# A residual gate's matrix-vector product moved from TensorE to VectorE, and a branch projection split in two, in a hybrid block on one core

## The chip, the cores and the metric

One core of one Trainium2 chip runs the whole block in one launch. The metric is device microseconds of one execution: the median of the kernel before is 1565.91 us (three runs, 1564.96 to 1569.58).

## The reference

One layer (DEPTH is 1) over 256 context and 256 latent tokens with D_MODEL 2048. Only the latent stream is returned, so the context is used as keys, values and seed states alone. Cut to what matters here:

```
shift, scale, gate = split(silu(c) @ w_mod + b_mod, 3)          # c is one vector of 2048
h      = rms_norm(x) * (1 + scale) + shift                      # 512 tokens, context first
parts  = split(h @ w_in)                                        # 3 mixers' inputs, 3 x 2048 merge logits
y_na   = neighbourhood attention, 16 heads of 64                # latent queries, latent and context keys
y_pool = multiscale pooling, 4 channel groups of 256
y_rw   = RWKV-7 scans in both directions, 16 heads of 64, latent seeded by context
b_i    = y_i * silu(gate_i)                                     # 256 x 1024 each, i = 0, 1, 2
merged = sum over i of sigmoid(logits_i) * (b_i @ w_branch[i])  # 1024 -> 2048
out    = rms_norm(x + gate * (merged @ w_out)) * final_g
```

All is fp32. The residual gate is a product of one vector of 2048 with a 2048 x 2048 part of w_mod (16.8 MB), plus a bias.

## The kernel before

There are three stages. The first (up to about 150 us of the profiled execution) computes shift and scale, turns x, builds h in 16 K tiles (`hh`, `hl`) and already multiplies seven column tiles. The second ("mixers", to about 1470 us) does all else up to `merged`. The third multiplies by w_out and writes the result.

Matrix products of fp32 numbers are made of three products each: a number is split into a rounded high part (cast on ScalarE, L576) and a remainder (subtraction on VectorE, L577), and high x high, low x high, high x low are accumulated (`mm3`, L580 to L584, and L856).

In the mixers weights are read in units of 512 KB (`load_unit`, three `raw` buffers); a unit is split in two halves (`split_half`, five buffers for each part), and every half gives some matmuls. There are four kinds of work for these units. `column_tile` (L835) multiplies h with 128 columns of w_in: queries, keys, values and gates of a pair of attention heads, inputs and gates of the pooling and of a pair of RWKV heads. `merge_group` (L955), twelve of them, multiplies the latent part of h with 512 columns of the merge logits over 16 K tiles (96 matmuls of 512 columns), takes a tanh (half of the sigmoid) and stores it in DRAM (`md_`). `branch_group` (L959), three branches by four column groups, multiplies a branch's output, 8 K tiles (48 matmuls), with w_branch, and multiplies in the merge gate, which it reads back from `md_` (`gates_in`, with the third of its four units). The branch outputs go to DRAM (`bs`, by `keep`, L882) and come back as K tiles in the places of hh and hl when h isn't needed any more (`branch_load`, L618). The fourth kind are the gate units.

`gate_units` (L1105) computes the residual gate: 32 units of eight matmul instructions. Each multiplies a [128, 32] tile of `cs` (the two conditioning vectors and zeros) with 256 columns of the gate's weights (`wg`, loads of 256 KB) for four K tiles, each in a column group of its own of the array. A matmul with the matrix `selg` (L1100) then sums the four groups over partitions and spreads the row over 128 partitions, the bias is added, and the result goes to DRAM (`gd`) until the last stage.

`Order` (L447) writes out TensorE's order by hand, as a plan of the program in which every piece of work has a cost in us and streams have due times: the attention and pooling of the pairs one after the other (`side`, first priority), the last sums' transposes (`turn`), and the RWKV pairs (`rwkv`), in which features, a triangular inverse (VectorE), an 8-step chain and a readout follow each other, and the next pair's start overlaps. After at most 2.2 us of streams comes at least 0.6 us of units. Units are prepared three halves ahead. `todo` (L1137) lists the tiles in their order, each with the event it waits for; the first that is free is taken, and a merge group always is (the last one is held back until nothing else is left). The tiles of attention pair p wait for `side{p-1}`. When `todo` is empty come the branch groups, in order; those of the third branch wait for `rw7`, the output of the last RWKV pair. Gate units are added to two of three halves once `side7` is there. The framework that lowers the program orders the other engines' instructions and the loads (nearly all DMAs are issued from SP) and puts in the waits.

Of the kernel before, what the change touches and what calls it, by code (L numbers as in the profile page):

```python
# [446 lines left out]
class Order:  # L447
# [48 lines left out]
    def run(s, units, most, least):  # L496

        while True:
            s.bursts(most)
            n = 0.0  # L500
            while n < least:
# [5 lines left out]
                if u is None:  # L507
                    nxt = [x[1] for x in s.streams if x[2] is None] + [s.ev[x[2]] for x in s.streams if x[2] in s.ev]
# [7 lines left out]
D = 2048  # L516
# [13 lines left out]
def hybrid_block(ctx, tc, x, cx, w_ms, w_st, w_in, w_mg, w_br, w_out, pool_w, icnt, wa, bias, rows, params, out, dbg=None):  # L530
# [81 lines left out]
    def branch_st(br):  # L612
        def st(k):
            c = slice(256 * (k % 2), 256 * (k % 2) + 256)
            return hh[4 * br + k // 2][:, c], hl[4 * br + k // 2][:, c]
        return st

    def branch_load(i):  # L618

        br, k = i // 4, 2 * (i % 4)  # L620
        for e, y in enumerate((hh, hl)):
            x = y[i] = hp.tile([P, 512], F32R, tag=f"h{'hl'[e]}{i}", name=f"b{'hl'[e]}{i}")
            nc.sync.dma_start(x.bitcast(F32).rearrange("p (k t) -> p k t", k=2), bs[br, e, k:k + 2].rearrange("k p t -> p k t"))

    def branch_src(br, c):
        return lambda u: w_br[br, 4 * c:4 * c + 4, :, 256 * u:256 * u + 256].rearrange("n p c -> p n c")
# [6 lines left out]
    sums = {}  # L633
# [17 lines left out]
    with ExitStack() as sx:  # L651
# [11 lines left out]
        selg = cp.tile([P, P], F32, name="selg")  # L663
        nc.gpsimd.memset(selg, 0.0)
        for g in range(4):
            r = slice(32 * g, 32 * g + 32)
            nc.gpsimd.affine_select(out=selg[r], in_=selg[r], pattern=[[0, P]], compare_op=ALU.not_equal, fill=1.0,
                                    base=-1, channel_multiplier=1)
# [197 lines left out]
    with ExitStack() as mx:  # L866
# [7 lines left out]
        T = {}  # L874
# [7 lines left out]
        def keep(br, p, b):  # L882
# [4 lines left out]
            nc.sync.dma_start(bs[br, 0, p], h.bitcast(F32))  # L887
            nc.sync.dma_start(bs[br, 1, p], l.bitcast(F32))
# [61 lines left out]
        def merge_out(i, t, d):  # L950
            th = wp.tile([P, 512], F32, tag="mt", bufs=2, name=f"mth{i}_{t}")
            nc.scalar.activation(th, d, AF.Tanh, scale=0.5)  # L952
            nc.sync.dma_start(md_[i, t], th)
# [5 lines left out]
        def branch_group(br, c):  # L959
            th = {}  # L960

            def gates_in(u):
                for t in range(2):
                    th[t] = wp.tile([P, 512], F32, tag="mt", bufs=2, name=f"bth{br}_{c}_{t}")
                    nc.sync.dma_start(th[t], md_[4 * br + c, t])
                return u()

            def done(t, a):
                o = merged(t, c) if br == 0 else th[t]
                nc.vector.scalar_tensor_tensor(o, th[t], 1.0, a, ALU.add, ALU.mult)  # L970
                if br:
                    nc.vector.tensor_tensor(merged(t, c), merged(t, c), o, ALU.add)
# [4 lines left out]
            return us  # L977

        def turn(c):
            yield 0.0, 2.0  # L980
# [5 lines left out]
        def rwkv(p):  # L986
# [33 lines left out]
            keep(2, p, g)  # L1020
            O.mark(f"rw{p}")
# [74 lines left out]
        def gate_out(cc, gs, gb):  # L1096
            yield 0.0, 1.2
            c = slice(512 * cc, 512 * cc + 512)
# [6 lines left out]
        def gate_units():  # L1105

            held = []

            def load(cc, h, k):
                wg = np_.tile([P, 2, 256], F32, tag=("kt", "sl")[k // 2 % 2], bufs=2 + k // 2 % 2, name=f"wg{cc}_{h}_{k}")  # L1110
                nc.sync.dma_start(wg, w_mg[cc, k, :, :, 256 * h:256 * h + 256])
                held.append(wg)
                if k % 2 == 0:
                    return []

                def mult():
                    if h == 0 and k == 1:
                        T["mg"] = psn.tile([P, 512], F32, tag="s", name=f"mg{cc}")
# [221 lines left out]
```

## Time and profile before

| | |
|---|---|
| median of 3 runs | 1565.91 us |
| profiled execution | 1570.13 us, span 1568.4 us |
| TensorE matmul busy | 1509.2 us (96%), 12248 instructions |
| VectorE busy | 1129.1 us (72%), 2588 instructions |
| ScalarE busy | 798.9 us (51%), 1597 instructions |
| GpSimd busy | 243.5 us (16%), 436 instructions |
| DMA | 289.26 MB, mean 184 GB/s |
| chain that ended last | PE 81%, DVE 7%, DMA 5%, ACT 4%, issue 3% |

PE is TensorE, DVE VectorE, ACT ScalarE, POOL GpSimd, SP the engine that issues most DMAs. Busy times of an engine are shares of the span from its first to its last instruction; matmuls are pipelined, so that their durations overlap. The chain follows the last instruction back, at each step to what released it.

### The profile page before, as it was taken

What the parts mean: (1) busy time and instruction counts of PE and PEld (TensorE: products, weight loads), DVE (VectorE), ACT (ScalarE), POOL (GpSimd) and SP (SyncE); (2) the same over time, 40 slices, a digit from 0 to 9 for tenths busy, and PEclk for the clock granted to TensorE, in tenths of its full rate; (3) what the DMA queues carried; (4) which work ended last, traced back from release to release, by engine and by line L of the source; (5) the groups of instructions that cost most, each with busy time, mean ns of one, the idle gap of its engine ahead of it and who ended that gap; (6) DMA issues with size and microseconds to landing.
All of it is one profiled execution on the core that took longest, in us unless ns stands there. A gap on an engine that the chain in (4) does not pass through costs nothing.

```text
span 1568.4 us, 32279 instructions
## 1 busy us (share of the span) xinstructions
PE 1509.2 (96%) x12248; PEld 1197.0 (76%) x12248; DVE 1129.1 (72%) x2588; ACT 798.9 (51%) x1597; POOL 243.5 (16%) x436
## 2 busy tenths in 40 slices
PE   6999999999999999999999999999999997999998
PEld 4667778788877897788789877877896664666787
DVE  4334688788788777886887778768877775666674
ACT  5224563566365546544664556446646642334553
POOL 2222010040023023201230130023023200210000
PEclk9999999999999999999999999999999999999999
DMA  9996445555543464344355524623566698877863
GB/s 391 348 330 219 143 135 169 146 160 182 159 144 98 132 177 148 100 132 121 99 165 164 166 90 123 189 103 112 172 193 217 193 309 260 273 253 250 285 220 106
DMA packets 218380, 289.26 MB, mean 184 GB/s; under 512 B 62576, under 2 KB 176368, under 8 KB 213616
## 3 DMA queue, kind: packets, MB, share of 16 engines
q1 hardware_dynamic: 218224, 287.20, 57.1%
q8 instruction: 96, 1.57, 0.4%
q14 instruction: 60, 0.49, 0.1%
HBM read 265.38 MB, written 21.50 MB: 183 GB/s over the span
## 4 chain that ended last, share of the span: by engine, by line
PE 81%; DVE 7%; DMA 5%; ACT 4%; issue 3%; SPq 0%; ACTq 0%; POOL 0%; DVEq 0%; POOLq 0%
PE d L856 32%; PE dg L582 8%; PE dg L583 7%; PE dg L584 7%; PE acc L780 2%; PE o L584 2%; PE o L582 2%; PE o L583 2%; DVE wlo L577 2%; PE px L374 1%; PE pu L388 1%; PE acc L786 1%; PE acc L783 1%; PE pS L398 1%; DMA raw<-in_w_br 1%
## 5 line engine op out<-in xcount | busy, mean ns | idle before, releaser
L576 ACT CAST whi<-raw 128x512 fp32r<-128x512 f32 x584 | 355.1, 619 | 395.0 <-PE d L856 163.5
L577 DVE TENSOR_TENSOR wlo<-raw,whi 128x512 fp32r<-128x512 f32 x584 | 401.1, 698 | 142.2 <-ACT whi L576 113.7
L856 PE MATMUL d<-hh,whi 128*128 128x256 f32 (+1 forms) x1184 | 366.5, 329 | 0.9 <-ACT mth L952 0.9
L856 PE MATMUL d<-hl,whi 128*128 128x256 f32 (+1 forms) x1184 | 358.1, 322 | 0.0
L856 PEld LDWEIGHTS d<-hh,whi 128*128 128x128 f32 x1184 | 224.8, 190 | 24.1 <-issue 2.9
L856 PE MATMUL d<-hh,wlo 128*128 128x256 f32 (+1 forms) x1184 | 241.4, 323 | 0.0
L856 PEld LDWEIGHTS d<-hl,whi 128*128 128x128 f32 x1184 | 225.2, 190 | 16.2 <-issue 0.2
L856 PEld LDWEIGHTS d<-hh,wlo 128*128 128x128 f32 x1184 | 182.7, 190 | 17.0 <-issue 0.7
L582 PE MATMUL dg<-whi,hh 128*128 128x512 f32 x384 | 164.2, 428 | 5.4 <-DVE gnag L896 3.6
L370 POOL TENSOR_SCALAR sg<-SV,G 64x64 f32<-64x64 f32 x192 | 109.1, 574 | 362.1 <-DVE SV L407 201.0
L584 PE MATMUL dg<-wlo,hh 128*128 128x512 f32 x384 | 151.0, 393 | 0.3 <-DVE wlo L577 0.3
L583 PE MATMUL dg<-whi,hl 128*128 128x512 f32 x384 | 151.2, 394 | 0.0
L582 PE MATMUL dg<-whi,bh 128*128 128x512 f32 x192 | 83.9, 437 | 11.9 <-ACT whi L576 8.5
L582 PEld LDWEIGHTS dg<-whi,hh 128*128 128x128 f32 x384 | 72.1, 188 | 28.8 <-issue 5.3
L584 PEld LDWEIGHTS dg<-wlo,hh 128*128 128x128 f32 x384 | 72.4, 189 | 17.2 <-DVE wlo L577 0.7
L583 PEld LDWEIGHTS dg<-whi,hl 128*128 128x128 f32 x384 | 72.6, 189 | 9.8
L584 PE MATMUL dg<-wlo,bh 128*128 128x512 f32 x192 | 77.2, 402 | 1.4 <-DVE wlo L577 1.4
L583 PE MATMUL dg<-whi,bl 128*128 128x512 f32 x192 | 77.0, 401 | 0.8 <-DMA bl<-bs 0.8
L309 DVE TENSOR_TENSOR iM<-iA,iT 128x126 f32<-128x126 f32 (+22 forms) x248 | 63.3, 255 | 12.9 <-DMA iA<-dA 6.5
L311 DVE TENSOR_TENSOR iT<-iT,iM 128x126 f32<-128x126 f32 (+22 forms) x248 | 63.2, 255 | 6.7
L793 ACT ACTIVATE hh<-xT,md 128x256 fp32r<-128x256 f32 x32 | 17.5, 593 | 88.1 <-DVE md L708 88.1
L582 PEld LDWEIGHTS dg<-whi,bh 128*128 128x128 f32 x192 | 37.0, 192 | 30.6 <-ACT whi L576 12.0
(323 smaller groups left out, 2480.0 us busy)
## 6 DMA issues: line engine op xcount, KB each, us to landing
raw<-in_w_in SPq DMA_DIRECT2D x244, 512.0 KB, 3.7
wm<-in_w_ms SPq DMA_DIRECT2D x32, 1024.0 KB, 5.9
raw<-in_w_br SPq DMA_DIRECT2D x48, 512.0 KB, 5.2
wg<-in_w_mg SPq DMA_DIRECT2D x64, 256.0 KB, 4.4
raw<-in_w_out SPq DMA_DIRECT2D x32, 512.0 KB, 4.3
wst<-in_w_st SPq DMA_DIRECT2D x16, 448.0 KB, 7.1
md__79<-mth SPq DMA_DIRECT2D x24, 256.0 KB, 3.0
bth<-md__79 SPq DMA_DIRECT2D x24, 256.0 KB, 3.7
```

The costliest lines, as they stand in the source:

```text
L309: nc.vector.tensor_tensor(m, A[:, st:st + 1, st + 1:32].to_broadcast([128, ni, nt]), T[:, 0:ni, st:st + 1].to_broadcast([128, ni, nt]), AL ...
L311: nc.vector.tensor_tensor(T[:, 0:ni, st + 1:32], T[:, 0:ni, st + 1:32], m, ALU.add)
L370: nc.gpsimd.tensor_scalar(sg[hv[par], d], SV[hv[par], par, w, d], G[hv[par], gs[d][0], d:d + 1], None, ALU.mult)
L374: nc.tensor.matmul(px[hv[par], d], EO[:, par, d, cs[d], :], SV[:, par, w, d], start=True, stop=True, tile_position=(0, 64 * par))
L576: nc.scalar.copy(hi, src)
L577: nc.vector.tensor_tensor(lo, src, hi.bitcast(F32), ALU.subtract)
L582: nc.tensor.matmul(acc, a[0], b[0], start=start, stop=False)
L583: nc.tensor.matmul(acc, a[1], b[0], start=False, stop=False)
L584: nc.tensor.matmul(acc, a[0], b[1], start=False, stop=stop)
L780: mm = nc.tensor.matmul(acc[i], shi[:, c], hh[j], start=(j == 0), stop=False)
L793: nc.scalar.activation(hh[j][:, c], xT[:, j, c], AF.Identity, bias=mds[j][:, 0, e:e + 1], scale=mds[j][:, 1, e:e + 1])
L856: nc.tensor.matmul(box[0], w[m >= 8][:, 128 * i:128 * i + 128], x, start=(v == 0 and m == 0), stop=(v == 3 and m == 11))
```

## The change

The gate's products leave TensorE. `gate_piece` multiplies one K tile of 512 columns of the gate's weights by the conditioning value of each partition and adds it to a running [128, 512] sum: one operation on VectorE per K tile, 16 for a block of 512 columns, 64 in all, each with a load of 256 KB into one of two buffers (tag `kt`). A block is begun when the attention and pooling of pairs 1, 3, 5 and 7 are done (`side1`, ...), with one piece for every half unit. A matmul with a matrix of ones then sums over partitions and spreads. The attention tiles of pairs 2, 4 and 6 now wait for the block before them (`gate0` to `gate2`).

The third branch is projected in two parts of four K tiles: the first parts of all four column groups wait for `rw5`, the second ones for `rw7`. Each part is multiplied by the merge gate by itself and added; the additions of the second parts are on POOL but for the last group. The gate tiles for the second parts are fetched earlier into buffers that are free by then (`ahead`). `gates_in` comes with the last unit of a group instead of the third.

The last RWKV pair's output is split and stays in SBUF (`T["last"]`); K tile 7 of branch 3 is read from there. Operands of the third branch are loaded from `rw6` on, with every second unit. `gd`, `md_` and `bs` become separate DRAM tiles, and the stores of `md_` and of the high parts of `bs` are issued from ScalarE's queue.

```diff
-    gd = drp.tile([P, D], F32, name="gd")
-    md_ = drp.tile([12, 2, P, 512], F32, name="md_")
-    bs = drp.tile([3, 2, 8, P, NT], F32, name="bs")
+    gd = [drp.tile([P, 512], F32, name=f"gd{i}") for i in range(4)]
+    md_ = [drp.tile([2, P, 512], F32, name=f"md{i}_") for i in range(12)]
+    bs = [[drp.tile([2, P, NT], F32, name=f"bs{b}_{e}_{k}") for k in range(4)] for b in range(3) for e in range(2)]
...
-    def branch_st(br):
+    def branch_st(br, k0=0):
         def st(k):
+            k += k0
+            if br == 2 and k == 7:
+                return T["last"]
...
-            nc.sync.dma_start(bs[br, 0, p], h.bitcast(F32))
-            nc.sync.dma_start(bs[br, 1, p], l.bitcast(F32))
+            nc.scalar.dma_start(bs[2 * br][p // 2][p % 2], h.bitcast(F32))
+            nc.sync.dma_start(bs[2 * br + 1][p // 2][p % 2], l.bitcast(F32))
...
+            def ahead(u):
+                for t in range(2):
+                    tag, n = (("kt", 2), ("sl", 3), (("sl", 3), ("vT", 1))[t], ("mt", 2))[c]
+                    pool = wp if tag == "mt" else np_
+                    x = gates2[c, t] = pool.tile([P, 512], F32, tag=tag, bufs=n, name=f"cth{c}_{t}")
+                    nc.sync.dma_start(x, md_[8 + c][t])
+                return u()
...
+                    (nc.gpsimd if part == 2 and c < 3 else nc.vector).tensor_tensor(merged(t, c), merged(t, c), o, ALU.add)
-                if br == 2 and t and c < 3:
+                if part == 2 and t and c < 3:
                     O.add(turn(c), 1)
-            us = group(8, branch_src(br, c), branch_st(br), done)
-            us[2] = lambda u=us[2]: gates_in(u)
+            if part == 2:
+                us = group(4, branch_src(br, c, 2), branch_st(br, 4), done)
+                if c == 3:
+                    us[0] = lambda u=us[0]: ahead(u)
+                return us
+            us = group(4 if part else 8, branch_src(br, c), branch_st(br), done)
+            us[-1] = lambda u=us[-1]: gates_in(u)
+            if part and c < 3:
+                us[1] = lambda u=us[1]: ahead(u)
             return us
...
+            if p < 7:
+                keep(2, p, g)
+            else:
+                h = wp.tile([P, NT], F32R, tag="th", bufs=1, name="lasth")
+                l = np_.tile([P, NT], F32R, tag="ql", name="lastl")
+                nc.scalar.copy(h, g)
+                nc.vector.tensor_tensor(l, g, h.bitcast(F32), ALU.subtract)
+                T["last"] = h, l
+            O.mark(f"rw{p}", 1.5 * (p == 7))
...
+        def gate_out(cc, gs):
+            gb = np_.tile([P, 512], F32, tag="vT", name=f"gb{cc}")
+            nc.sync.dma_start(gb, rows[0:1, 512 * cc:512 * cc + 512].to_broadcast([P, 512]))
+            yield 0.0, 2.0
             pg = psn.tile([P, 512], F32, tag="o", name=f"pg{cc}")
-            nc.tensor.matmul(pg, selg, gs, start=True, stop=True)
+            nc.tensor.matmul(pg, ones, gs, start=True, stop=True)
             nc.vector.tensor_tensor(gb, pg, gb, ALU.add)
-            nc.sync.dma_start(gd[:, c], gb)
+            nc.sync.dma_start(gd[cc], gb)
             yield 1.1, 0.0
+            O.mark(f"gate{cc}")
+        def gate_piece(cc, kt):
+            wg = np_.tile([P, 512], F32, tag="kt", bufs=2, name=f"wg{cc}_{kt}")
+            nc.sync.dma_start(wg, w_mg[cc, kt // 2, :, kt % 2])
+            if kt == 0:
+                gs[cc] = np_.tile([P, 512], F32, tag="sl", bufs=3, name=f"gs{cc}")
+                nc.vector.tensor_scalar(gs[cc], wg, cs[:, kt, 1:2], None, ALU.mult)
+            else:
+                nc.vector.scalar_tensor_tensor(gs[cc], wg, cs[:, kt, 1:2], gs[cc], ALU.mult, ALU.add)
+            if kt == 15:
+                O.add(gate_out(cc, gs[cc]), 1)
...
-            na = f"side{p - 1}" if p else None
+            na = (f"gate{p // 2 - 1}" if p % 2 == 0 else f"side{p - 1}") if p else None
...
-        late = [(br, c) for br in range(3) for c in range(4)]
+        late = [(br, c) for br in range(2) for c in range(4)] + [(2, c, part) for part in (1, 2) for c in range(4)]
...
-                            elif not todo and late and (late[0][0] < 2 or O.has("rw7")):
+                            elif not todo and late and (len(late[0]) < 3 or O.has(("rw5", "rw7")[late[0][2] - 1])):
...
-                            if last >= 18 and loads and O.has("rw7"):
+                            if last >= 18 and last % 2 == 0 and loads and O.has("rw6"):
                                 branch_load(loads.pop(0))
...
-                    if n % 3 and O.has("side7") and gates and not 4 <= (last or 0) < 9:
-                        ready[-1] = ready[-1] + gates.pop(0)()
+                    if gates and O.has(f"side{2 * gates[0][0] + 1}"):
+                        gate_piece(*gates.pop(0))
```

## Rows read from the trace of the kernel before

**Rows 1.** Windows by stage: us, busy (instructions) of PE, PEld, DVE, ACT, POOL; clock, DMA share, GB/s.

```profile
160.00:1160.00 1000.00, 981.81 (x8553) 813.60 (x8552) 795.01 (x1868) 558.02 (x1149) 163.63 (x323) 1.00 0.46 141
...
1260.00:1340.00 80.00, 69.17 (x470) 47.85 (x468) 50.58 (x122) 25.09 (x44) 0.00 (x0) 0.96 0.92 279
...
1420.00:1480.00 60.00, 56.19 (x248) 45.06 (x248) 41.06 (x72) 28.11 (x53) 0.00 (x0) 0.97 0.89 293
```

**Rows 2.** Instructions grouped by line, PE: busy us, mean ns; idle before.

```profile
L1123 PE MATMUL mg<-wg,cs 128*32 128x256 f32 x256 | 20.4, 391 | 0.0
```

**Rows 3.** Timeline of PE around one gate unit: start us, us, instruction.

```profile
1401.58 0.40 PE L584 MATMUL dg<-wlo,bh 128*128 128x512 f32 x1
1401.91 0.64 PE L1123 MATMUL mg<-wg,cs 128*32 128x256 f32 x8
1402.48 0.50 PE L582 MATMUL dg<-whi,bh 128*128 128x512 f32 x1
1402.82 0.40 PE L583 MATMUL dg<-whi,bl 128*128 128x512 f32 x1
1403.06 0.40 PE L584 MATMUL dg<-wlo,bh 128*128 128x512 f32 x1
1403.29 0.40 PE L582 MATMUL dg<-whi,bh 128*128 128x512 f32 x1
```

**Rows 4.** Timeline of PE, the longest wait: idle before and its releaser in brackets.

```profile
1321.85 0.80 PE L582 MATMUL dg<-whi,bh 128*128 128x512 f32 x1 [4.37 <-ACT whi L576]
```

**Rows 5.** Windows inside the late stretch.

```profile
1286.00:1300.00 14.00, 11.83 (x57) 7.66 (x58) 12.71 (x37) 4.57 (x8) 0.00 (x0) 1.00 1.02 333
...
1324.00:1332.00 8.00, 8.00 (x91) 5.72 (x91) 4.35 (x7) 2.89 (x6) 0.00 (x0) 0.77 0.86 261
```

**Rows 6.** Timeline of DVE and PE where the last RWKV pair ends.

```profile
1419.11 0.42 DVE L1019 SCALAR_TENSOR_TENSOR grwg<-y,grwg 128x256 f32<-128x256 f32 x1
...
1427.61 0.47 PE L582 MATMUL dg<-whi,bh 128*128 128x512 f32 x1 [1.28 <-ACT whi L576]
1428.90 0.50 PE L583 MATMUL dg<-whi,bl 128*128 128x512 f32 x1 [0.82 <-DMA bl<-bs]
```

**Rows 7.** Timeline of PE, SP and ACT at a border of two branch groups.

```profile
1445.86 0.47 PE L582 MATMUL dg<-whi,bh 128*128 128x512 f32 x1 [0.76 <-DVE bth L970]
...
1448.69 1.49 SPq L564 DMA_DIRECT2D raw<-in_w_br  x2
...
1453.87 1.16 ACT L576 CAST whi<-raw 128x512 fp32r<-128x512 f32 x2 [1.56 <-DMA raw<-in_w_br]
```

**Rows 8.** Timeline of DVE: three remainders in a row.

```profile
370.22 1.88 DVE L577 TENSOR_TENSOR wlo<-raw,whi 128x512 fp32r<-128x512 f32 x3
```

**Rows 9.** Windows of 35 to 44 us after each second attention pair's pooling.

```profile
357.00:392.00 35.00, 35.00 (x288) 28.66 (x287) 29.71 (x60) 21.94 (x44) 0.61 (x1) 1.00 0.61 185
593.00:634.00 41.00, 40.77 (x397) 32.05 (x397) 32.84 (x76) 26.46 (x56) 13.80 (x27) 1.00 0.47 147
866.00:910.00 44.00, 44.00 (x397) 34.65 (x396) 32.77 (x67) 24.89 (x50) 9.14 (x18) 1.00 0.52 170
1173.00:1215.00 42.00, 42.00 (x431) 29.10 (x433) 30.05 (x67) 25.96 (x53) 12.49 (x21) 1.00 0.70 224
```

**Rows 10.** Line L1111, the 64 loads of the gate's weights: time to landing.

```profile
DMA to landing us min/median/max: 3.0/4.4/7.9
```

**Rows 11.** Timeline of ACT: the last pooling tile's tanh, the next merge group's.

```profile
354.31 0.39 ACT L894 ACTIVATE thplg<-d 128x256 f32<-128x256 f32 x1
...
384.56 0.60 ACT L952 ACTIVATE mth<-dg 128x512 f32<-128x512 f32 x1 [0.63 <-PE dg L584]
```

**Rows 12.** Timeline of ACT: tanh of the ninth and tenth merge groups.

```profile
1100.95 1.09 ACT L952 ACTIVATE mth<-dg 128x512 f32<-128x512 f32 x2
...
1203.70 0.60 ACT L952 ACTIVATE mth<-dg 128x512 f32<-128x512 f32 x1 [0.47 <-PE dg L584]
```

**Rows 13.** Waits of SP: line, for whom, us in total, times, longest.

```profile
SPq L887 <- ACT kh L884: 48.7, 21, 6.0
```

More of the change, by code (lines that the diff above doesn't have):

```diff
@@ L507, in run @@
                 if u is None:
-                    nxt = [x[1] for x in s.streams if x[2] is None] + [s.ev[x[2]] for x in s.streams if x[2] in s.ev]
+                    nxt = [x[1] for x in s.streams if x[2] is None] + [s.ev[x[2]] for x in s.streams if x[2] in s.ev] \
+                        + [v for v in s.ev.values() if v > s.t] * (not s.streams)
                     assert nxt, [x[2] for x in s.streams]
@@ L632, in merged @@
         return sums[t, c]
-    sums = {}
+    sums, T = {}, {}
     mhl = {}
@@ L662, in hybrid_block @@
         nc.vector.tensor_tensor(cs[:, :, 1], csil[:, 16:32], pp[:, PC_C + 16:PC_C + 32], ALU.mult)
[L663 to L668, printed above, removed]
+        ones = cp.tile([P, P], F32, name="ones")
+        nc.gpsimd.memset(ones, 1.0)
         xT = xp.tile([P, 16, 512], F32, name="xT")
@@ L873, in hybrid_block @@
         O = Order(tc)
-        T = {}
         def ztile(tag, nm, n):
@@ L952, in merge_out @@
             nc.scalar.activation(th, d, AF.Tanh, scale=0.5)
-            nc.sync.dma_start(md_[i, t], th)
+            nc.scalar.dma_start(md_[i][t], th)
         def merge_group(i):
@@ L957, in merge_group, with branch_group @@
             return group(16, src, lambda k: (hh[k][:, 256:512], hl[k][:, 256:512]), lambda t, d: merge_out(i, t, d))
-        def branch_group(br, c):
+        def branch_group(br, c, part=0):
             th = {}
@@ L1101, in gate_out @@
             nc.vector.tensor_tensor(gb, pg, gb, ALU.add)
-            nc.sync.dma_start(gd[:, c], gb)
+            nc.sync.dma_start(gd[cc], gb)
             yield 1.1, 0.0
[L1105 to L1118, printed above, removed]
-                    a = T["mg"][:, 256 * h:256 * h + 256]
-                    for i in range(4):
-                        kt = 2 * k - 2 + i
-                        g = kt % 4
-                        nc.tensor.matmul(a[32 * g:32 * g + 32], cs[:, kt], held[i // 2][:, i % 2], start=(kt < 4), stop=(kt >= 12),
-                                         tile_position=(0, 32 * g), skip_group_check=True)
-                    del held[0:2]
-                    if h == 1 and k == 7:
-                        gs = np_.tile([P, 512], F32, tag="sl", bufs=3, name=f"gs{cc}")
-                        gb = np_.tile([P, 512], F32, tag="sl", bufs=3, name=f"gb{cc}")
-                        nc.scalar.copy(gs, T["mg"])
-                        nc.sync.dma_start(gb, rows[0:1, 512 * cc:512 * cc + 512].to_broadcast([P, 512]))
-                        O.add(gate_out(cc, gs, gb), 1)
-                    return 0.75
-                return [mult]
-            return [lambda cc=cc, h=h, k=k: load(cc, h, k) for cc in range(4) for h in range(2) for k in range(8)]
@@ new lines, in gate_out @@
+            O.mark(f"gate{cc}")
+        gs = {}
+        def gate_piece(cc, kt):
[8 more added lines that the diff above has]
+                O.add(gate_out(cc, gs[cc]), 1)
@@ L1162, in hybrid_block @@
             todo.append((None, lambda i=i: merge_group(i)))
-        late = [(br, c) for br in range(3) for c in range(4)]
+        late = [(br, c) for br in range(2) for c in range(4)] + [(2, c, part) for part in (1, 2) for c in range(4)]
         def units():
-            ready, halves, cur, gates = [], [], [], gate_units()
+            ready, halves, cur = [], [], []
+            gates = [(cc, kt) for cc in range(4) for kt in range(16)]
             n = 0
@@ L1252, in hybrid_block @@
         cs_ = slice(512 * cc, 512 * cc + 512)
-        late = ((gate[:, cs_], gd[:, cs_]), (xr[0][:, cs_], x[0:128, cs_]), (xr[1][:, cs_], x[128:256, cs_]),
+        late = ((gate[:, cs_], gd[cc]), (xr[0][:, cs_], x[0:128, cs_]), (xr[1][:, cs_], x[128:256, cs_]),
                 (fg[:, cs_], rows[1:2, cs_].to_broadcast([P, 512])))
```

25 lines of the change are left out of this document (12 added, 13 removed).

## The prediction

> **What bounds the kernel now.** I read the busy time by stage first. TensorE is busy for 981.8 of the 1000 us of the mixers, but for 69.2 of the 80 us from 1260 to 1340, and 56.2 of the 60 from 1420 to 1480 [rows 1]. The order of its instructions is fixed when the kernel is built, and it works through them in that order. So the time is its work plus its idle time, and a change earns what it takes from either. The idle time that lies late is the first thing to see: 10.8 us between 1260 and 1340, in the stretch in which the gate's weights (64 loads), the branch weights and the branch operands are all being fetched. There the DMA share is 0.92, and VectorE isn't full.
>
> **What the gate's products cost TensorE.** Of the group, the reader is to see 256 instructions, 391 ns each, and only 20.4 us busy [rows 2]: four column groups run at once, and each unit is eight instructions. The timeline gives the price of one unit. Between two products of a branch group lie 0.23 us from start to start (1403.06 to 1403.29); across a unit they lie 0.90 us apart (1401.58 to 1402.48), and the next one comes 0.34 instead of 0.23 us later [rows 3]. That is 0.67 + 0.11 = 0.78 us a unit, and 32 units make 25.0 us. The bounds are 20.4 (busy alone) and 25.0; I take 25.0, since starts hold the gaps too. The Trainium skill (Perfetto Trace Analysis, Identifying the Most-Contended Engine) warns that busy time of matmuls is a poor measure because they are pipelined. The trace agrees: the 256 durations add up to 100 us, the busy time is 20.4 and the starts say 25.0; by the busy time the sum below would gain 4.6 us less.
>
> The four sums over partitions stay (a matrix of ones instead of the selecting one, same shape): no change.
>
> **What the late stretch gives back.** The longest single wait of TensorE, 4.37 us ahead of 1321.9, is for the high part of a branch weight [rows 4], and the DMA share was 1.02, at 333 GB/s, from 1286 to 1300 [rows 5]. Three quarters of the gate's 16.8 MB leave this part of the kernel. Idle: 10.8 us. The clock was granted at 0.77 from 1324 to 1332, right after that idle time [rows 5]; 8 us x 0.23 = 1.8 us of work. Together 12.6 us go, if what replaces the gate loads doesn't saturate the queues again (below).
>
> **What the last pair's wait gives back.** TensorE waits 1.28 and 0.82 us at 1427 to 1429, the second for the operand read back from DRAM [rows 6]. With that operand in SBUF, and three of its four neighbours loaded from rw6 on, 2.1 us go. The split of the third branch adds no product: 4 groups of 8 K tiles become 8 of 4. It moves 4 x 24 products x 0.23 = 22 us ahead of the last pair. Without it, taking out 25 us of gate units would leave TensorE short of filler: the last chain's final product on VectorE starts at 1419.1 [rows 6], the second branch's fillers last to about 1427, so 8 us are left over; 8 + 22 - 25 = 5 us still are. Next late is then the chain of the last pair itself. Four more group borders, each with a wait like the 0.76 us at 1445.9 [rows 7], at most 3 us, at least 0; I take 1, as most borders show none.
>
> **What the pieces on VectorE cost.** 64 operations of 128x512, fp32; the nearest rows are the low parts of weights, three in 1.88 us, 0.63 each [rows 8]. 40 us of VectorE in four blocks of 16, 10.1 us a block. In the stretches where the blocks will fall (after the pooling of each second head pair) VectorE is busy 29.7 of 35, 32.8 of 41, 32.8 of 44 and 30.1 of 42 us [rows 9]. With 10.1 more the first is over by 4.8, the second by 1.9; the others fit. TensorE, which has no idle time there to give (35.0 of 35, 40.8 of 41), stalls for what is over, 6.7 us, and for chain steps that stand behind a piece on VectorE. The bounds are 0 (weights are split three halves ahead) and 39: a piece's load waits for the piece two before it, since two buffers hold them; a load lands in 4.4 us [rows 10], so two pieces take 4.4 + 0.63 = 5.0 us, 2.5 a half unit, and a merge group of 16 half units takes 30.2 us (354.3 to 384.6), 1.89 each [rows 11]; 64 x 0.61 = 39. I take 10, nearer to the full-engine count, because the late loads' 4.4 was measured where the queues are full. Behind a waiting load stand the weight loads on SP; behind a waiting piece, every chain step on VectorE.
>
> Moved by this: the tiles of head pairs 2, 4 and 6 wait for a block. A block is 16 half units, as long as a merge group, so each pair can come up to 30 us later, and merge groups fill in. Nine of the twelve are done at 1102, the tenth at about 1205 [rows 12], so there are just enough; cost 0, at worst one group short, 22 us (96 products x 0.23).
>
> **What the new order of loads costs.** In the first parts of branch 3 the gate tiles are fetched with the second of two units, behind the read of the group before. The rows of a group of today: first product at 1445.86, the weights' load behind the gate tiles' at 1448.69, their cast at 1453.87 [rows 7], so the unit behind the gates is ready 8.6 us after the border (0.6 for the cast). Today two units (5.5 us) and the turned sums cover that; then one unit does, 4 x 3 x 0.23 = 2.8 us. Bounds per group: 0 (the weights may be issued ahead, chain steps fill in) to 5.8; four groups, 0 to 23 us. I take 7, a third, since chain steps lie between there and the load will be faster with the gate's loads gone. In the eight groups of branches 1 and 2 the gates move to the last of four units, which is included in the 12.6.
>
> Branch operands (0.5 MB for every second unit), weights (0.5 MB a unit of 2.76 us) and gate tiles (0.5 MB a group of 11 us) still ask for about 95 + 190 + 47 = 332 GB/s, as much as the best stretch moved [rows 5]. Bounds 0 to 10.8; I take 4, for two groups instead of six.
>
> At nothing: stores issued on ACT (ACT is off the path; SP spent 48.7 us waiting ahead of the kept operands' stores alone [rows 13], hidden by three weight buffers; -3 to 3, the latter if the casts of weights come late behind them), six additions on POOL (hidden by the next group's products; the transposes behind them would wait some tenths more without these), DRAM tiles apart (0 to -2).
>
> **Sum.** Gone 25.0 + 12.6 + 2.1 = 39.7. Added 10 + 7 + 4 + 1 = 22. Net -17.7. The profiled execution took 1570.1 us (span 1568.4), 4.2 over the median 1565.9; I take the difference to the median: 1548.
>
> **Rivals.**
> *Clean (0.20).* The late waits go and none comes: VectorE 2, gates 0, queues 2, borders 1, so -34.7: 1531. For it: three halves of lead. Against: the first block's 35 us with only 5.3 us free.
> *Filler runs short (0.16).* One merge group missing before the seventh pair's tiles come, or the 5 us margin at the last pair gone: 10 to 22 us of idle on top of the forecast: 1558 to 1570. For it: nine of twelve used before 1102. Against: tiles of the other branch also become ready while a pair waits.
> *Slower: pieces set the pace (0.13).* SP and VectorE wait in turn for the two buffers; 39 instead of 10: +11, 1577. It decides from 0.43 us a piece on (17.7 + 10 over 64 pieces). For it: VectorE full in block one, a weight load queued behind each waiting piece. Against: the DMA share there is 0.47 to 0.70 [rows 9], so loads land faster.
> The forecast has 0.51.
>
> **How the numbers follow.** A measurement of this kernel tells about 0.3%, 4.7 us, from no change. The forecast and the clean case are faster; of the filler case a third is (below 1561) and the rest is the same; of the slower case a sixth is the same. Faster 0.51 + 0.20 + 0.05 = 0.76; same 0.11 + 0.02 = 0.13; slower 0.11. The forecast's own range is 1538 to 1558. The full one reaches into the clean case and into the filler case: 1526 to 1566, with 0.07 below and 0.13 above.
>
> **What would show it.** Right: no matmuls on the gate's weights, TensorE busy down by 20 or more; idle from the end of the seventh pair's pooling to the last pair below half of today's 10.8; no wait for an operand read back. VectorE near full in the blocks with TensorE idle 1 to 5 us each. Wrong: idle of over 25 us in the mixers, loads of the gate's weights that wait long on SP, TensorE idle at the borders of branch 3's first parts for over 4 us each, or idle just ahead of the second parts.

## The result, and the profile after

The changed kernel takes 1582.22 us (median of 4 runs, 1576.43 to 1582.80) against 1567.35 of the kernel before on the same chip (1564.96 to 1569.58): ratio 1.0087, interval 1.0058 to 1.0116. It is slower; 1548 was predicted, and 1582 lies above the range. The profiled execution of the changed kernel took 1576.43 us, its span is 1574.7; it is the fastest of the four, so its trace shows rather too little of the loss than too much.

TensorE's busy time fell by 12.8 us, from 1509.2 to 1496.4. That is less than the 20 or more that was forecast, at a mean granted clock of 0.985 instead of 0.993. More idle time came in its place: 1574.7 - 1496.4 = 78.3 us against 59.2 before. The page of the changed kernel, its busy times and its chain:

```profile
PE 1496.4 (95%) x11992; PEld 1204.0 (76%) x11992; DVE 1179.8 (75%) x2662; ACT 794.9 (50%) x1591; POOL 258.9 (16%) x438
...
PE 69%; DVE 13%; DMA 7%; ACT 4%; issue 4%; POOL 1%; SPq 1%; ACTq 0%; DVEq 0%; POOLq 0%
```

In the chain VectorE has 13% where it had 7%, and TensorE 69% where it had 81%. Where the idle time is, the windows of the changed kernel say (us; busy of PE, PEld, DVE, ACT, POOL; clock, DMA share, GB/s). The first three answer to [rows 1]; the next four are the blocks of gate pieces, which answer to [rows 9] (the third block's last pieces run on to 989.8); then come the three stretches between blocks.

```profile
160.00:1160.00 1000.00, 967.04 (x8271) 793.35 (x8270) 805.79 (x1847) 541.89 (x1118) 163.79 (x310) 0.99 0.49 152
1260.00:1340.00 80.00, 66.61 (x408) 52.77 (x408) 69.28 (x165) 35.14 (x63) 2.13 (x2) 0.91 0.85 274
1420.00:1480.00 60.00, 56.97 (x293) 44.11 (x292) 53.96 (x96) 30.16 (x58) 9.26 (x6) 1.00 0.77 252
...
325.00:400.00 75.00, 68.19 (x667) 56.95 (x666) 66.87 (x134) 40.96 (x88) 16.12 (x28) 0.98 0.65 204
600.00:645.00 45.00, 40.12 (x329) 28.43 (x328) 40.12 (x87) 24.79 (x52) 14.62 (x25) 0.92 0.65 210
915.00:965.00 50.00, 43.78 (x473) 37.51 (x473) 41.35 (x89) 26.54 (x60) 24.70 (x40) 0.93 0.56 180
1240.00:1320.00 80.00, 64.46 (x489) 53.12 (x488) 65.81 (x142) 38.11 (x76) 17.59 (x23) 0.89 0.72 229
...
400.00:600.00 200.00, 197.17 (x1775) 166.08 (x1774) 158.74 (x395) 101.90 (x211) 28.65 (x56) 1.00 0.47 147
645.00:915.00 270.00, 265.83 (x2224) 216.82 (x2222) 212.11 (x499) 147.38 (x300) 38.31 (x77) 0.99 0.43 133
965.00:1240.00 275.00, 271.15 (x2352) 222.75 (x2349) 216.70 (x515) 148.12 (x301) 34.95 (x74) 0.99 0.47 145
```

The four blocks hold 6.8 + 4.9 + 6.2 + 15.5 = 33.4 us of idle TensorE in 250 us; the 745 us between them hold 10.9. From 160 to 1160 the idle time is 33.0 us, where it was 18.2 [rows 1]: over 25 us there was one of the prediction's own signs of being wrong. In three of the blocks the granted clock is 0.89 to 0.93 besides. VectorE is busy for 82 to 89% there, not full.

What waits can be seen on the lines of the pieces in the changed kernel (busy us, mean ns; idle time of the engine just before them, and what ended it):

```profile
L1147 DVE SCALAR_TENSOR_TENSOR gs<-wg,cs,gs 128x512 f32<-128x512 f32 x60 | 44.7, 745 | 18.1 <-DMA wg<-in_w_mg 17.4 <-DVE sq L103 0.4
L1145 DVE TENSOR_SCALAR gs<-wg,cs 128x512 f32<-128x512 f32 x4 | 3.5, 880 | 5.3 <-POOL px L946 5.3
L1131 PE MATMUL pg<-gs,ones 128*128 128x512 f32 x8 | 5.5, 769 | 10.6 <-DVE gs L1147 10.5
```

VectorE stands 17.4 us for the loads of its next piece (13 of the 64 pieces wait) and 5.3 for a buffer that GpSimd still reads; TensorE stands 10.5 us for the sums over partitions (8.4 of them once, in the last block). What is queued behind a piece on VectorE stands too, as the order of the next rows shows. The timeline of VectorE in the third block of the changed kernel, with TensorE's below it:

```profile
928.68 0.98 DVE L1145 TENSOR_SCALAR gs<-wg,cs 128x512 f32<-128x512 f32 x1 [2.29 <-POOL px L946]
929.59 1.23 DVE L578 TENSOR_TENSOR wlo<-raw,whi 128x512 fp32r<-128x512 f32 x1
930.75 0.99 DVE L405 SCALAR_TENSOR_TENSOR SV<-pS,G,sg 64x64 f32<-64x64 f32 x4
935.38 0.75 DVE L1147 SCALAR_TENSOR_TENSOR gs<-wg,cs,gs 128x512 f32<-128x512 f32 x1 [3.65 <-DMA wg<-in_w_mg]
936.16 0.29 DVE L377 COPY xs<-px 128x128 f32<-128x128 f32 x1
```

```profile
927.50 0.45 PE L398 MATMUL pS<-SV,BKT 128*64 128x64 f32 x8 [1.48 <-ACT SV L390]
931.78 0.45 PE L374 MATMUL px<-SV,EO 128*64 128x64 f32 x8 [1.60 <-DVE SV L405]
936.51 0.69 PE L388 MATMUL pu<-xs,AT 64*64 64x64 f32 x8 [2.11 <-DVE xs L377]
```

The copy `xs`, a step of the RWKV chain, takes 0.29 us; it could have run about 3 us earlier, but a piece that waits 3.65 us for its load is ahead of it. TensorE, whose order is fixed, waits 2.11 us for that copy. None of this makes VectorE look full.

### The profile page after: what moved, and what is told of

Same layout as the page of the kernel before. It is cut to its first block, busy times and chain, and to the rows that moved or that the text cites. A ratio compares the mean times of both kernels' runs of the same rounds, so it can differ in the third digit from the quotient of the medians.

```text
span 1574.7 us, 31809 instructions
## 1 busy us (share of the span) xinstructions
PE 1496.4 (95%) x11992; PEld 1204.0 (76%) x11992; DVE 1179.8 (75%) x2662; ACT 794.9 (50%) x1591; POOL 258.9 (16%) x438
## 4 chain that ended last, share of the span: by engine, by line
PE 69%; DVE 13%; DMA 7%; ACT 4%; issue 4%; POOL 1%; SPq 1%; ACTq 0%; DVEq 0%; POOLq 0%
PE d L860 27%; PE dg L583 7%; PE dg L584 6%; PE dg L585 6%; DVE wlo L578 3%; DMA wg<-in_w_mg 3%; PE o L583 2%; PE o L585 2%; PE o L584 2%; PE acc L784 2%; DMA raw<-in_w_br 2%; PE acc L790 1%; PE acc L787 1%; ACT whi L577 1%; PE px L374 1%
## 5 line engine op out<-in xcount | busy, mean ns | idle before, releaser
L370 POOL TENSOR_SCALAR sg<-SV,G 64x64 f32<-64x64 f32 x192 | 112.7, 593 | 379.2 <-DVE SV L407 204.0
L584 PEld LDWEIGHTS dg<-whi,hl 128*128 128x128 f32 x384 | 73.9, 193 | 10.5 <-issue 0.2
L583 PE MATMUL dg<-whi,bh 128*128 128x512 f32 x184 | 77.1, 419 | 4.9 <-DVE cth L984 1.9
L585 PE MATMUL dg<-wlo,bh 128*128 128x512 f32 x184 | 72.7, 395 | 0.0
L584 PE MATMUL dg<-whi,bl 128*128 128x512 f32 x184 | 72.5, 394 | 0.0
L1285 DVE TENSOR_TENSOR wl<-raw,wh 128x512 fp32r<-128x512 f32 x64 | 42.3, 704 | 22.4 <-ACT wh L1284 22.3
```

The lines of the kernel that those rows point to most:

```text
L370: nc.gpsimd.tensor_scalar(sg[hv[par], d], SV[hv[par], par, w, d], G[hv[par], gs[d][0], d:d + 1], None, ALU.mult)
L583: nc.tensor.matmul(acc, a[0], b[0], start=start, stop=False)
L584: nc.tensor.matmul(acc, a[1], b[0], start=False, stop=False)
L585: nc.tensor.matmul(acc, a[0], b[1], start=False, stop=stop)
L1285: nc.vector.tensor_tensor(l, r, h.bitcast(F32), ALU.subtract)
```

## The experiments

Theory 1: the pieces' place costs the time (waits of VectorE for a load or a buffer, with the chain behind them). Theory 2: VectorE's 48 us of additional work do. Theory 3: the other parts of the change do. All kernels are the changed one with the edit shown in brief, unless said otherwise; e1, e2, e8, e12, e16 and e17 leave out the gate or compute it from wrong data, so they are measurements and not versions to use; ratios are to the kernel before, in the same batch of runs, and "us" of a difference is the difference of ratios times 1567.35.

**The pieces left out, in part or whole.**

```diff
 e1_no_pieces, in gate_piece
-            wg = ...; nc.sync.dma_start(wg, ...); (products)
+            if kt == 0: nc.vector.memset(gs[cc], 0.0)
 e2_no_loads
-            wg = np_.tile(..., tag="kt", bufs=2); nc.sync.dma_start(wg, ...)
+            wg = lt[kt % 2].bitcast(F32)
 e3_late_sum, in gate_out
-            yield 0.0, 2.0
+            yield 0.0, 12.0
 e4_pe_gate: selg, gate_units, gate_out, the rule n % 3 and na = side{p-1} as before
```

> The changed kernel with the gate's 64 loads and 64 products left out (each block's sum is a tile of zeros), its four marks, its four sums over the partitions and everything else kept; the gate in the output is left out. Theory 1 (the pieces' place: in four dense blocks, in two buffers that pooling still reads, behind their own loads, ahead of the heads' chain on an in-order VectorE) and theory 2 (the 47 us of VectorE work itself): the four blocks' 33 us of idle TensorE fall to the 4 us that the stretches between them show over the same length, and some 10 us of low clock go: 1540, between 1533 and 1550. Theory 3 (the other parts of the change, the split third branch and the stores on the ScalarE queue, cost the time): 1573 to 1582.

> The changed kernel with all 64 products on VectorE, but out of a tile that is in SBUF anyway, without the 64 loads and their two buffers; the gate's values are wrong data. Theory 1 (waits for loads and for buffers that GpSimd still reads): most of the loss goes, 1542 to 1556, at most 10 us above the kernel without pieces. Theory 2 (VectorE's own work): 1570 to 1582, within 12 us of the changed kernel.

> The changed kernel with the sum over the partitions planned 12 us after the last product in place of 2. The waits of TensorE for that sum's operand (10.5 us in three) should go. Theory 1: 1568 to 1575 (10 us less, up to 4 more by a better clock in the last block). Theory 2 (VectorE is late anyway, and the next matmul that needs it waits as long): 1578 to 1584.

> The gate's products back on TensorE as in the kernel before, with all else of the change kept (third branch in two parts, last pair's operands in SBUF, separate DRAM tiles, stores on the ScalarE queue). Theories 1 and 2 (the pieces alone cost the time): 1555 to 1567, at or under the kernel before. Theory 3 (the other parts cost): above 1572.

| | median us | ratio | interval |
|---|---|---|---|
| changed | 1582.22 | 1.0087 | 1.0058 to 1.0116 |
| e1_no_pieces | 1549.32 | 0.9886 | 0.9858 to 0.9915 |
| e2_no_loads | 1562.84 | 0.9977 | 0.9960 to 0.9995 |
| e3_late_sum | 1603.18 | 1.0242 | 1.0221 to 1.0263 |
| e4_pe_gate | 1570.70 | 1.0027 | 1.0008 to 1.0046 |

Theory 3 falls: without the pieces the rest of the change gains 18 us (1549.3, at the upper end of its range). With the gate's products back on TensorE the rest gains nothing (it costs 1 to 7 us), which neither theory had expected. Products without loads cost 14 us, and the loads 17 more: e2_no_loads came out between the ranges of theories 1 and 2, and each has about half.

The later sum was a miss of both theories: 24 us worse. The sums' waits went (10.5 to 1.2 us). But the next pair's tiles wait for the gate's mark, and the last pooling's products come at 1296 instead of 1272 (before: 1173). Two windows of e3_late_sum:

```profile
1200.00:1260.00 60.00, 49.31 (x651) 41.45 (x649) 42.59 (x104) 32.86 (x80) 15.17 (x34) 0.89 0.23 74
1320.00:1400.00 80.00, 69.90 (x421) 51.59 (x421) 54.91 (x128) 27.05 (x48) 5.07 (x8) 0.91 0.89 283
```

In the first, TensorE is idle for 10.7 of 60 us with the DMA share at 0.23, as there is little left to load for: no tanh of a merge group stands between 1143.3 and 1326.0, so all groups but the last are used up. Then the branches come at once, and the DMA share is 0.89. That is the rival "filler runs short" of the prediction, in another kernel.

**The block mended, the pieces spread, and the floor.**

```diff
 e5_mended_block
+    tag, n = (("kt", 2), ("kt", 2), ("vT", 1))[kt % 3]; product of kt - 2 with the load of kt
+    O.mark(f"gblk{p}", 4.0)          # a block waits for this mark
-            yield 0.0, 2.0
+            yield 0.0, 12.0
 e6_spread: na = side{p-1}; gs is the memory of cs, set to the bias row / 128 first
+    gflat = cs.rearrange("p a b -> p (a b)")
+    wgs[cc, kt] = wp.tile([P, 512], F32, tag="mt", bufs=2)
+    m = n % 6;  m == 0: gate_load(...);  m == 3: gate_piece(...)
 e7_spread_on_before: the same spread in the kernel before
 e8_no_gate: no loads, products or sums; na = side{p-1}
```

> The changed kernel with its four blocks kept, but each block's first load 4 us later, three buffers in place of two, each product two halves after its load, and the sum planned 12 us after the last product: the waits for loads and for pooling's buffers go, and the heads of the next pair start some 20 us later. If the waits of VectorE set the cost (19.5 us between the changed kernel and the one without loads): 1560 to 1568. If it is the time at which the next pair of heads may start (the kernel with the later sum lost 21 us by that): 1590 to 1615, above the changed kernel.

> The 64 products still on VectorE with all else of the change, but one for every six halves of weight tiles over the whole of the mixers: the running sum in a tile of its own (that of the modulation operand, no longer needed), the loads three halves ahead of their products in the buffers of the merge tanh, no tile waiting for a gate. If the dense blocks are the cause: the kernel with the gate on TensorE less its 25 us, and up to 8 more for 47 us of spread VectorE work: 1546 to 1554, 1 per cent faster than the kernel before. If VectorE's own work costs wherever it stands (13.5 us measured without loads, or more): 1559 to 1570, no gain.

> The same spread products put alone into the kernel before: third branch whole, last pair through DRAM, stores on the SyncE queue. The kernel before less 25 us and up to 8 more: 1542 to 1551. If the split third branch and the rest cost something (3 us measured with the gate on TensorE), this is 2 to 6 us under the spread with all else of the change; if they gain once the gate is off TensorE, it is 5 or more above it.

> The changed kernel with the gate left out altogether (no loads, no products, no sums over the partitions; the stored gate is the row alone), and no tile waiting for a gate: the floor for the change. If holding the next pair of heads back behind a gate costs by itself: 1538 to 1545, 4 to 11 us under the kernel that left out only the loads and products. If it costs nothing: 1547 to 1551, as that kernel.

| | median us | ratio | interval |
|---|---|---|---|
| e5_mended_block | 1610.20 | 1.0263 | 1.0232 to 1.0293 |
| e6_spread | 1571.81 | 1.0028 | 1.0007 to 1.0048 |
| e7_spread_on_before | 1588.78 | 1.0132 | 1.0100 to 1.0163 |
| e8_no_gate | 1544.57 | 0.9844 | 0.9819 to 0.9869 |

The mended block held the next pair back (the last pooling's products come at 1304) and lost, as e3 did. The spread missed its 1550 by 22 us: dense blocks alone aren't the cause. The floor, with no gate at all, is 24 us under the kernel before. It is also 7 us under e1_no_pieces (ratios 0.9844 and 0.9886, intervals that overlap a little): that is what the four sums and the hold on the next pair cost together, and no run separates the two.

The spread in the kernel before was to be 1542 to 1551 and is 16 us slower than the spread with the rest of the change (ratios 1.0132 and 1.0028). Its TensorE, at the last pair:

```profile
1453.19 0.77 PE L582 MATMUL dg<-whi,bh 128*128 128x512 f32 x1 [6.63 <-DMA bh<-bs]
1455.03 0.79 PE L583 MATMUL dg<-whi,bl 128*128 128x512 f32 x1 [1.07 <-DMA bl<-bs]
```

So once the gate is off TensorE, the rest of the change (the third branch in two parts, the last operands in SBUF, the stores on ScalarE's queue, all together) is worth 16 us; with the gate on TensorE it is worth nothing. The read-back of the last pair is a part of it: from 1420 to 1480 TensorE is idle for 12.4 us at a clock of 0.86 in e7, and for 3.2 at 1.00 in e6. But from 160 to 1160 it is idle for 39.9 us in e7 against 30.6 as well, so the late stretch isn't all, and which part of the change gives how much was not tested.

**Is it the loads of the spread, or its products?**

```diff
 e9_spread_poolq (e9 to e12 are e6_spread with the edit shown)
-            nc.sync.dma_start(wgs[cc, kt], w_mg...)
+            nc.gpsimd.dma_start(wgs[cc, kt], w_mg...)
 e10_spread_own: 128 pieces of 256 columns, every third half
+            wgs[cc, kt] = np_.tile([P, 256], F32, tag="wg", bufs=1)
+            nc.tensor.matmul(pg, one[:, 0:1].to_broadcast([P, P]), gflat, ...)
 e11_spread_ahead
-            m == 3: gate_piece
+            m == 5: gate_piece
 e12_spread_no_loads
-            wgs[cc, kt] = wp.tile(...); nc.sync.dma_start(...)
+            wgs[cc, kt] = lt[kt % 2].bitcast(F32)
```

> The spread products with their 64 loads issued from GpSimd's queue and not from SyncE's. In the spread kernel SyncE's queue stood before these loads for the merge buffers (some 25 us in waits for the stores of the merge tanh) and for products, with the weight loads and the heads' DRAM round trips behind it. If that queue is what the spread products cost: 1550 to 1560. If VectorE's work is: 1568 to 1574, no change. If GpSimd's own work to issue the loads disturbs the chain: above 1575.

> The spread products as 128 pieces of 256 columns, one for every three halves, loaded into a buffer of their own (1 KB a partition; room is made by reading the column of ones with a stride of zero), so that no load waits for a merge store and no merge tanh for a product. If the shared buffers cost the time: 1552 to 1562. If the number of VectorE instructions and their work does: 1570 to 1580 (128 products of some 0.4 us are 51 us against 48).

> The spread products with each load five halves ahead of its product in place of three, all else the same. If VectorE's waits for loads (14.9 us in 12) cost the time: 1558 to 1564. If the merge buffers do, which are now held for two halves longer: 1572 to 1580.

> The spread products without their 64 loads, out of a tile that is in SBUF anyway (the gate's values are wrong data). If the loads, their buffers and the queue are the cost of the spread kernel: 1546 to 1554, at most 9 us above the kernel without a gate. If VectorE's work is, wherever it stands: 1564 to 1573.

| | median us | ratio | interval |
|---|---|---|---|
| e9_spread_poolq | 1607.41 | 1.0235 | 1.0207 to 1.0264 |
| e10_spread_own | 1576.96 | 1.0048 | 1.0031 to 1.0065 |
| e11_spread_ahead | 1581.63 | 1.0081 | 1.0061 to 1.0101 |
| e12_spread_no_loads | 1567.77 | 0.9984 | 0.9966 to 1.0001 |

Without loads the spread is 22 us above the floor, with them 29: here the products on VectorE, with the four sums, are most of the price, some 0.3 us a product. Three attempts to make the loads cheaper lost. Products two halves later (e11) hardly shortened VectorE's waits for loads (14.1 us against 14.9) and cost 8 us. Issued by GpSimd the loads were worst; two of its waits (line, for whom, us, times, longest):

```profile
POOL wg L1142 <- ACT whi L577: 88.5, 3, 52.6
...
POOL wg L1142 <- DVE cs L1150: 59.2, 18, 8.7
```

GpSimd stands before its loads (256.4 us in all), late loads make VectorE stand (46.0 us in 27 waits, against 14.9 in 12), and the chain's own steps on GpSimd are queued behind; how the loss of 32 us divides between these was not tested. Buffers of their own with half the width made two products of 485 ns out of one of some 750, and VectorE waited 39.2 us for the single buffer's loads.

**What of the block is the loads'.** Between e2_no_loads and the changed kernel lie 17 us.

```diff
 e13_block_other_buffers: blocks and hold as changed; loads into "mt", gs in cs as in e6_spread; each product one step after its load
 e14_block_no_hold: e13 with na = side{p-1}, sum 6 us after
 e15_half_rate: e14 with one piece for every two halves
 e16_loads_unused: after the load
+            wg = lt[kt % 2].bitcast(F32)
 e17_loads_alone: loads as changed, no products
 e18_block_prefetched: e5 with the sum 2 us after and no 4 us: three buffers, product of kt - 2
```

> The four dense blocks at the same places and with the same hold on the next pair as in the changed kernel, but loaded into the buffers of the merge tanh, and summed in the tile of the modulation operand, so that nothing of a block shares a buffer with pooling or the attention tiles. If the buffers that pooling still reads are what the loads cost (19.4 us lie between the changed kernel and the one without loads): 1563 to 1569. If it is the landing of each load one or two buffers ahead: 1575 to 1583.

> The same dense blocks in those other buffers, but no pair of heads waits for them any more; the sum is planned 6 us after the last product. If holding the pairs back is what makes a block dear: 1552 to 1560. If VectorE's order does: 1562 to 1572, no gain over the spread kernel.

> As the dense blocks without a hold, but one product for every two halves: between the dense blocks and the spread. If each product costs the same wherever it stands (some 0.3 us): 1562 to 1572, as these two. If crowding costs: under the dense blocks by 4 us or more.

> The changed kernel with its 64 loads at their places and its 64 products at theirs, but the products read a tile that is in SBUF anyway, so that VectorE never waits for a load (the gate's values are wrong data). Between this one and the kernel without loads (1562.8) lies what the loads cost by the DMA queue and the memory; between this one and the changed kernel (1582) what VectorE's waits for them cost. If VectorE's waits on an in-order queue set the cost: 1563 to 1568. If SyncE's queue and the weight loads behind do: 1575 to 1582.

> The changed kernel with its 64 loads but no products (the blocks' sums are zeros; the gate in the output is left out). If the loads by themselves cost nothing: 1549 to 1553, as the kernel without loads and products (1549.3). If they delay the weights behind them on SyncE's queue: 1556 to 1568.

> The changed kernel's dense blocks with three buffers in place of two and each product two halves after its load; the block begins as soon as in the changed kernel and the sum is planned 2 us after the last product, so the next pair is held back by two halves more and not by 16 us. If VectorE's waits for loads are the 19.4 us: 1565 to 1574. If loads and weights collide on the queue, or the longer hold eats it: 1578 to 1590.

| | median us | ratio | interval |
|---|---|---|---|
| e13_block_other_buffers | 1583.24 | 1.0099 | 1.0077 to 1.0120 |
| e14_block_no_hold | 1581.45 | 1.0085 | 1.0062 to 1.0108 |
| e15_half_rate | 1576.54 | 1.0061 | 1.0045 to 1.0077 |
| e16_loads_unused | 1562.36 | 0.9964 | 0.9951 to 0.9976 |
| e17_loads_alone | 1562.44 | 0.9954 | 0.9933 to 0.9975 |
| e18_block_prefetched | 1568.38 | 0.9990 | 0.9976 to 1.0004 |

Taking away the buffers shared with pooling (e13) and then the hold (e14) left the time as it was. This alone doesn't clear them: in the new buffers SyncE stood 32.0 and 25.3 us for the merge gates' stores, and e14 missed both its ranges. What e13, e14 and e15 have in common with the changed kernel is VectorE's wait for loads, 15.3, 13.8 and 13.5 us; half the rate (e15) gained some 4 us over e14, with intervals that overlap, and missed its range as well.

With all 64 loads and all 64 products, but no product waiting for its load, it is 1562.4, the same as with no loads at all. The pieces' line of e16_loads_unused:

```profile
L1148 DVE SCALAR_TENSOR_TENSOR gs<-lt,cs,gs 128x512 f32<-128x512 f32 x60 | 45.4, 756 | 0.7
```

So 19 us of the changed kernel hang on VectorE's waits for loads. Two things go with these waits in e16 and belong to the 19: TensorE no longer waits for the sums (0.0 us against 10.5), and a load no longer waits for the product that holds its buffer. The latter is a rival, since SyncE then holds the weights' loads back, but the numbers speak against it: SyncE stands ahead of the gate's loads for 81.6 us in e16 and 94.6 in the changed kernel, and in e18_block_prefetched, where loads still wait for products (31.5 us, 29.7 in the changed kernel), most of the loss went all the same. That kernel is the mended block without the longer hold, and confirms it from the other side; here its pieces' line, and three of its blocks:

```profile
L1158 DVE SCALAR_TENSOR_TENSOR gs<-wg,cs,gs 128x512 f32<-128x512 f32 x60 | 44.8, 746 | 4.0 <-DMA wg<-in_w_mg 3.9
```

```profile
325.00:400.00 75.00, 71.38 (x699) 59.61 (x699) 68.68 (x139) 42.86 (x93) 19.81 (x33) 0.98 0.67 209
600.00:645.00 45.00, 42.31 (x359) 30.88 (x357) 39.68 (x84) 25.58 (x55) 16.45 (x26) 0.96 0.69 220
1240.00:1320.00 80.00, 72.16 (x503) 56.91 (x501) 70.82 (x153) 40.33 (x81) 12.76 (x16) 0.98 0.84 264
```

Its third block lies earlier, from 895.5 to 951.2; from 890 to 990 TensorE is idle for 5.2 us in e18 and 6.3 in the changed kernel. The products are as long as in the changed kernel (746 ns) and as many, the waits for loads are 3.9 instead of 17.4 us, and the idle time of these four stretches is 3.6 + 2.7 + 5.2 + 7.8 = 19.3 us instead of 33.5, at a better clock. The kernel is then 15 us faster than the changed one, and no different from the kernel before. No version that computes the gate beat the kernel before.

What stays open is the rest: loads alone cost 11 us over no pieces (0.9954 against 0.9886), products alone 14, and both together, unlinked, 12. They don't add up, and no run says why. e17_loads_alone lies in the range that was given for weights delayed behind these loads, and SyncE stands ahead of them for 87.9 us there; that this is their price was not tested.

## Why the prediction was wrong, by its steps

*The pieces on VectorE: 10 us, measured 31.5* (ratios 1.0087 and 0.9886, with and without). This step failed. I counted VectorE's busy time against the length of the stretch and priced what was over. The blocks show that VectorE had 11 to 18% of the time left and TensorE stood all the same. The prediction had the waits in its "slower" rival, with 0.13: a load waits for the piece two before it, the next piece for the load, from 0.43 us a piece on. It measured 31.5 / 64 = 0.49 us, and the time, 1582, is near the rival's 1577. The kind of wait was right there, but that the number came near is in part luck. The rival let every piece come 2.5 us after the last, against 1.89 us a half unit. In the changed kernel only 13 pieces waited for a load, and the blocks took 50 to 61 us, 3.1 to 3.8 us a piece; in e16_loads_unused, with nothing to wait for, they still took 49 to 58. So the 1.89, read where one merge group ran, doesn't hold in the blocks, and a block isn't as long as a merge group (30 us). What costs is the single wait with a chain step behind it. I chose against the bound because the loads would land faster where the queues aren't full. They hardly did: 3.8 us (median) for the changed kernel's loads against 4.4 [rows 10]:

```profile
DMA to landing us min/median/max: 2.5/3.8/6.5
```

Of the 31.5 us, 19 hang on waits for loads (e16_loads_unused), and the other 12 are there in a kernel where no piece waits for its load; their cause stays open. The 0.63 us per piece read from remainders [rows 8] was too little as well: 0.745 us, 64 times, are 48 us and not 40.

*The wait for the sum over partitions: priced at nothing ("no change"), 10.5 us.* These lie within the 31.5 and not beside them, and go when the pieces are on time (0.0 in e16_loads_unused, 0.5 in e18_block_prefetched). The matrix had the same shape, but the sum came 2.0 us after the last piece by the plan, and the pieces ran late. In the last block (timeline of TensorE of the changed kernel, then two windows):

```profile
1314.31 2.08 PE L1131 MATMUL pg<-gs,ones 128*128 128x512 f32 x2 [8.40 <-DVE gs L1147]
...
1318.32 0.63 PE L585 MATMUL dg<-wlo,bh 128*128 128x512 f32 x1
1318.75 0.56 PE L583 MATMUL dg<-whi,bh 128*128 128x512 f32 x1
1319.14 0.39 PE L584 MATMUL dg<-whi,bl 128*128 128x512 f32 x1
1319.38 0.40 PE L585 MATMUL dg<-wlo,bh 128*128 128x512 f32 x1
1319.61 0.40 PE L583 MATMUL dg<-whi,bh 128*128 128x512 f32 x1
```

```profile
1314.00:1319.00 5.00, 4.69 (x9) 3.08 (x10) 4.66 (x16) 0.62 (x1) 0.00 (x0) 0.50 0.88 297
1319.00:1324.00 5.00, 5.00 (x23) 4.07 (x23) 4.64 (x14) 2.49 (x4) 0.00 (x0) 0.99 0.92 308
```

After the 8.4 us the granted clock is 0.50, its lower level of 1.2 GHz, for some 5 us: products start 0.43 us apart, then 0.23. A wait is paid a second time in this way.

*The units on TensorE: 25.0 gone.* In e1_no_pieces TensorE is busy for 1488.9 us, 20.3 less than before, at a mean clock of 0.991 instead of 0.993, which is about 3 us of these 1489. So by this estimate 23 went at equal clock: about right.

*The late stretch (12.6) and the last pair (2.1), less gates, queues and borders (7 + 4 + 1): net 2.7 gone.* TensorE's idle time in e1_no_pieces is 1548.5 - 1488.9 = 59.6 us, 59.2 before: nothing net. From 1260 to 1340 it is still idle for 8.0 us there, at a clock of 0.94, against 10.8 at 0.96 [rows 1]. The gate's loads had gone from that stretch, and the idle time mostly stayed. In this kernel the seventh pair comes later (last pooling product at 1252 instead of 1173), and its work falls into the stretch, but that isn't the main reason: in e8_no_gate that product comes at 1177, and 6.2 us stay idle, with the DMA share at 0.89. In the changed kernel the fourth block falls into it too, with 13.4 us idle. In the changed kernel the wait for the operand that was read back is gone, as predicted [rows 6].

The two together: the pieces cost 21.5 more than forecast and the rest gained 18 instead of 27.7, 10 less. That is 31 of the 34 us between 1548 and 1582; the other 3 are between the medians and the ratio (the kernel before was 1.4 us slower in this batch).

*The held pairs: cost 0.* In the changed kernel no stretch without filler shows: from 1320 to 1480 TensorE is idle for 5.8 us, 6.9 before. The floor leaves up to 7 us for the hold and the sums together. It held narrowly; with the sum planned 10 us later at each block the kernel lost 24 us.

## What to carry to other kernels

Work that is moved to an engine that also carries a chain costs by what is queued behind it while it waits, and not only by how full the engine is: give each load a lead of two pieces and a buffer that is free, before counting on idle time (here 15 us, with as many products and loads). A later product alone isn't enough: with buffers shared with the merge gates it left the waits at 14.1 us (e11_spread_ahead). Work on an engine at 75 to 80% that also carries steps of a dependent chain isn't free either: 48 us without a single long wait for a load cost 14 us in blocks, and 22 spread out (over a floor that has no sums either). And parts of a change can depend on each other: all that was changed beside the gate was worth 16 us with the gate spread on VectorE, and nothing with it on TensorE.

## What the runs showed of the hardware

A product of 256 columns on VectorE took 485 ns (mean of 128, e10_spread_own), one of 512 columns 745 (60 in the changed kernel): two halves take 225 ns more than one whole. Loads issued by GpSimd cost it time of its own: 292.2 us busy against 255.2 with the same loads on SyncE's queue, 0.6 us a load. And in TensorE's single wait of 8.4 us the granted clock fell from 1.00 (1300 to 1306 us) to 0.50 (1310 to 1314), and was back at 0.99 from 1319 to 1324.
